# Two-layer hybrid decoder trunk on one core: order of the seven products of the down-projection, place of its residual loads and one operand, and place of the rotary swap

## The chip, the cores and the metric

The kernel runs on one core of a Trainium2 chip, as one launch. The metric is the device time of the whole kernel in microseconds; lower is better. The engines are named PE (TensorE), DVE (VectorE), ACT (ScalarE), POOL (GpSimd) and SP (SyncE); "issue" of a DMA is the instruction on an engine's queue that starts it.

## The reference

A trunk of two layers on 1024 tokens of width 1024, all in float32. Per layer:

```python
proj = x @ w_in                      # u_pool, q, k, v, xc, gate_b, gate_c, gate_logits
q, k = partial_rope(q), partial_rope(k)   # first 16 of the 64 channels of each head
merged = sigmoid gates x (pool mixer, window attention, short conv)
x = layer_norm(ALPHA * x + merged @ w_o)
up = causal_dwconv(x @ w_up);  a, b = split(up)
x = layer_norm(ALPHA * x + (silu(a) * b) @ w_down)     # D_FF = 2816
```

## The kernel before, in words

Every float32 operand is split into a high and a low part (`split`, L87-94: the high part is a cast on ACT, L90; the low part a subtraction on DVE or POOL, L94), and every product is three matmuls (L110, L111, L112). The large matrix products are done in the Winograd form of Strassen's scheme, with seven half-size products in place of eight. Matmuls are 128 x 128 by 128 x 512.

The order of PE and SP is the written one. DVE, ACT and POOL are put in order by a scheduler that weighs priorities; `with self.urgent()` raises the priority of what is issued in it. Buffers come from pools with a fixed count of slots by name (X 14, t 6, s 3, pt 3, q 1, ws 3, w 6): a tile waits until the last reader of its slot is done.

`project` (the in-projection) runs pairs of output blocks, `pair` (L690). Each pair is `begin` (two of its seven products of 12 matmuls) and `rest` (five). In a pair, ACT copies products out of PSUM for the combinations: L724 copies product 1 before product 3 goes on in the same bank, L749 and L753 copy products 3 and 4, L756 product 5. L735 and L738 on POOL make the weight combinations. At the end `then` gets the two finished blocks. For keys and queries `then` is `turn` (L376): it puts `rotate` one tick later and `parts` two ticks later (`later`, ticks counted in pairs, `due` called after `begin`). `rotate` (L336) copies the block on ACT (L340), moves 8 rows four times with DMAs on ACT's queue (L342, L343) and does three operations on DVE (L344 to L346). Pairs of queries hold two such blocks.

`feed_forward` does the up-projection pairs, writes the hidden state to DRAM as the seven left operands of the down-projection (`h_blocks`, POOL and SP queues), then calls `down` (L823). `down` has seven products A11, A12, S2, S1, S3, S4, A22 (`plan`), each of 11 steps `j`, each step of 4 query blocks `q` with 3 matmuls. `operands` loads one step's 256 KB of h_blocks and its weights on SP into staging tiles that go round ws, X, s, makes differences on POOL in S2 (L861 to L863, kept for later products; `t2` is kept for A22) and splits. S1 and S3 use what S2 kept. A22 loads a weight and subtracts it from `t2` on POOL (L871). In the sixth and seventh product odd steps have their low part made on POOL. Steps late in A22 are held and run block by block at the end, so that the first block ends early.

Four banks `bank_a` hold A11 and then S2, S3, A22, four banks `bank_x` A12, S1, S4. After each product `reads` adds its banks into the residual rows `y` (eight tiles of 128 tokens by 1024 in float32, loaded from DRAM, L919, in one go after A11's step 6). Even token tiles are complete after S4, odd ones after A22; `finish` (L932) then calls `norm` (L262: statistics L259 and L267 on DVE, L290 on DVE, L291 on ACT, L292 on POOL or DVE). In layer 0 the normalised tiles are transposed by PE (`to_first`, `to_second`, L298 and following) as operands of the next projection, through the list `pend`; in layer 1 they are stored.

## Time and profile before

| | |
|---|---|
| time, median of 3 runs | 2821.2 us (2819.21 to 2821.59) |
| profiled execution | 2816.18 us, span 2814.4 us |
| granted PE clock, mean | 0.959 |
| busy share PE / DVE / POOL / ACT | 92% / 67% / 52% / 44% |
| DMA | 389.59 MB, mean 138 GB/s |
| first matmuls of the products, layer 0 (A11, A12, S2, S1, S3, S4, A22) | 1145.9, 1191.2, 1221.1, 1260.3, 1290.2, 1320.1, 1350.1 us |
| the same, layer 1 | 2545.1, 2592.1, 2622.0, 2661.1, 2691.1, 2721.0, 2757.8 us |
| first matmul of the second projection; last matmul of all | 1418.7; 2804.7 us |

Times within the trace count from the start of the span. A row of a stretch gives its length, each engine's busy time with the count of its instructions, the clock that the throttle granted to PE (1 is full speed), the mean busy share of the 16 DMA engines and what they moved. A row of waits names the waiting instruction, the one that released it, the sum, the count and the longest.

### The profile page before, as it was taken

What the parts mean: (1) busy time and instruction counts of PE and PEld (TensorE: products, weight loads), DVE (VectorE), ACT (ScalarE), POOL (GpSimd) and SP (SyncE); (2) the same over time, 40 slices, a digit from 0 to 9 for tenths busy, and PEclk for the clock granted to TensorE, in tenths of its full rate; (3) what the DMA queues carried; (4) which work ended last, traced back from release to release, by engine and by line L of the source; (5) the groups of instructions that cost most, each with busy time, mean ns of one, the idle gap of its engine ahead of it and who ended that gap; (6) DMA issues with size and microseconds to landing.
All of it is one profiled execution on the core that took longest, in us unless ns stands there. A gap on an engine that the chain in (4) does not pass through costs nothing.

```text
span 2814.4 us, 31939 instructions
## 1 busy us (share of the span) xinstructions
PE 2596.4 (92%) x11408; PEld 2118.0 (75%) x11408; DVE 1876.6 (67%) x2273; ACT 1228.1 (44%) x2005; POOL 1466.5 (52%) x959
## 2 busy tenths in 40 slices
PE   5989999999899999899689899989988999998996
PEld 4867887787688887678478678877876888876784
DVE  6465556747887877585474755567478887774847
ACT  4434445523544554334344344445235455543333
POOL 3444555666366655171643534666664556641723
PEclk7989999999999999999799999999999999998998
DMA  3433348554133333665223333575632333337552
GB/s 120 136 98 105 120 166 229 164 177 163 57 102 112 113 106 112 239 209 168 98 90 116 103 105 106 206 210 158 205 120 75 99 107 102 113 105 257 198 168 98
DMA packets 162896, 389.59 MB, mean 138 GB/s; under 512 B 17024, under 2 KB 48512, under 8 KB 161712
## 3 DMA queue, kind: packets, MB, share of 16 engines
q1 hardware_dynamic: 136496, 293.02, 32.2%
q0 software_dynamic: 14944, 55.19, 6.8%
q10 hardware_dynamic: 11296, 39.35, 3.7%
q8 instruction: 89, 1.46, 0.2%
q14 instruction: 71, 0.58, 0.1%
HBM read 281.75 MB, written 104.43 MB: 137 GB/s over the span
## 4 chain that ended last, share of the span: by engine, by line
PE 31%; DVE 7%; issue 4%; POOL 4%; ACT 2%; DMA 2%; SPq 0%; ACTq 0%; DVEq 0%; POOLq 0%
PE b L111 10%; PE b L112 10%; PE b L110 10%; DVE w L94 1%; DVE X L94 1%; ACT s L507 1%; DVE ve L275 1%; ACT w L90 0%; POOL ws L735 0%; POOL X L861 0%; POOL w L94 0%; ACT X L90 0%; POOL X L863 0%; DVE st L259 0%; DVE m L498 0%
## 5 line engine op out<-in xcount | busy, mean ns | idle before, releaser
L110 PE MATMUL b<-X,w 128*128 128x512 f32 x2552 | 1016.4, 398 | 56.9 <-ACT s L724 18.5
L112 PE MATMUL b<-X,w 128*128 128x512 f32 x2552 | 1009.6, 396 | 27.6 <-DVE w L94 19.3
L111 PE MATMUL b<-X,w 128*128 128x512 f32 x2552 | 1008.0, 395 | 3.4 <-DVE X L94 3.2
L94 DVE TENSOR_TENSOR w<-ws,w 128x512 fp32r<-128x512 f32 (+1 forms) x449 | 466.8, 1043 | 357.4 <-ACT w L90 342.9
L90 ACT CAST w<-ws 128x512 fp32r<-128x512 f32 (+1 forms) x605 | 409.0, 682 | 484.3 <-PE b L112 161.4
L110 PEld LDWEIGHTS b<-X,w 128*128 128x128 f32 x2552 | 488.8, 192 | 169.3 <-ACT s L724 21.9
L112 PEld LDWEIGHTS b<-X,w 128*128 128x128 f32 x2552 | 487.9, 191 | 135.7 <-DVE w L94 22.5
L111 PEld LDWEIGHTS b<-X,w 128*128 128x128 f32 x2552 | 488.8, 192 | 106.6 <-DVE X L94 5.8
L94 POOL TENSOR_TENSOR w<-ws,w 128x512 fp32r<-128x512 f32 (+1 forms) x156 | 307.4, 1973 | 427.5 <-ACT w L90 425.3
L738 POOL TENSOR_TENSOR ql<-ws 128x512 f32<-128x512 f32 x82 | 125.2, 1527 | 348.9 <-DMA ws<-in_w_in 256.5
L111 PE MATMUL b<-w,w 128*128 128x512 f32 x528 | 215.3, 408 | 37.4 <-DVE w L94 29.6
L110 PE MATMUL b<-w 128*128 128x512 f32 x528 | 212.2, 402 | 28.2 <-ACT w L90 28.2
L112 PE MATMUL b<-w,w 128*128 128x512 f32 x528 | 211.6, 401 | 0.0
L94 DVE TENSOR_TENSOR w<-X,w 128x512 fp32r<-128x512 f32 (+1 forms) x106 | 114.6, 1102 | 84.6 <-ACT w L90 80.6
L111 PEld LDWEIGHTS b<-w,w 128*128 128x128 f32 x528 | 102.9, 195 | 69.0 <-DVE w L94 39.2
L735 POOL TENSOR_TENSOR ws<-ws,ws 128x512 f32<-128x512 f32 x82 | 141.8, 1729 | 5.9
L110 PEld LDWEIGHTS b<-w 128*128 128x128 f32 x528 | 102.8, 195 | 52.4 <-ACT w L90 30.3
L800 DVE SCALAR_TENSOR_TENSOR q<-t,par,q 128x1023 f32<-128x1023 f32 x88 | 126.8, 1441 | 16.2 <-ACT q L797 15.1
L90 ACT CAST w<-X 128x512 fp32r<-128x512 f32 (+1 forms) x110 | 75.5, 704 | 130.3 <-PE b L112 63.9
L735 POOL TENSOR_TENSOR ws<-ql,ws 128x512 f32<-128x512 f32 x82 | 123.5, 1507 | 6.3
L800 DVE SCALAR_TENSOR_TENSOR pt<-t,par,pt 128x1023 f32<-128x1023 f32 x88 | 122.1, 1388 | 0.3
L735 POOL TENSOR_TENSOR ws<-ws 128x512 f32<-128x512 f32 x82 | 118.8, 1449 | 5.2 <-DVE w L94 0.7
(247 smaller groups left out, 3760.3 us busy)
## 6 DMA issues: line engine op xcount, KB each, us to landing
ws<-in_w_up SPq DMA_DIRECT2D x88, 512.0 KB
ws<-in_w_in SPq DMA_DIRECT2D x75, 512.0 KB
gates<-t ACTq DMA_DIRECT2D x48, 512.0 KB
ws<-in_w_o SPq DMA_DIRECT2D x40, 512.0 KB
h_blocks<-t SPq DMA_DIRECT2D x80, 256.0 KB
t<-gates SPq DMA_DIRECT2D x32, 512.0 KB
t<-q_parts POOLq DMA_DIRECT2D x64, 256.0 KB, 4.2
h_blocks<-pt SPq DMA_DIRECT2D x60, 256.0 KB
```

The costliest lines, as they stand in the source:

```text
L90: self.nc.scalar.copy(hi, src)
L94: return eng.tensor_tensor(lo, src, hi.bitcast(F32), op=ALU.subtract)
L110: self.nc.tensor.matmul(out, wh, xh, start=start and i == 0, stop=False, skip_group_check=more)
L111: self.nc.tensor.matmul(out, wh, xl, start=False, stop=False, skip_group_check=more)
L112: self.nc.tensor.matmul(out, wl, xh, start=False, stop=stop and i == n - 1, skip_group_check=more)
L275: nc.vector.scalar_tensor_tensor(ve[:], ve[:], r[:], r[:], op0=ALU.mult, op1=ALU.mult)
L507: nc.scalar.activation(p[:, j, 0:nk], pss[j // 2][:, j % 2], AF.Exp, bias=m[:, j:j + 1], scale=SCALE, accum_out=den[:, j:j + 1])
L735: sub = lambda out, x, y: nc.gpsimd.tensor_tensor(out, x, y, op=ALU.subtract)
L738: nc.gpsimd.tensor_tensor(s1[:], a21, a22, op=ALU.add)
L800: nc.vector.scalar_tensor_tensor(y[:, d:], c[:, :S - d], w(k), y[:, d:], op0=ALU.mult, op1=ALU.add)
```

## The change

Seven edits, all in one diff.

1. The rope tables: the negation goes from DVE to ACT, and the three stores of the table rows from POOL's queue to ACT's.
2. `rotate` is cut in two. `swapped` (the ACT copy and the four DMAs) is issued at the end of `rest`; the DVE part two ticks later and `parts` three ticks later. Ticks are now counted in `due`, which is called after each `begin` and after each `rest`. The other delayed calls keep their places, but for the table spread, which comes half a pair sooner.
3. S3 and S4 change places in `plan`: A11, A12, S2, S1, S4, S3, A22. Even token tiles are complete after the fifth product, and their norm is issued there.
4. A22's right operand is made in S1: `t2` minus the weight on POOL, in place, with the weight's load. A22 then loads only h_blocks. The split of an operand in two halves now goes to POOL too in odd steps of the sixth and seventh product.
5. The residual rows are loaded one after each of A12's first eight steps, and the add of A11's banks into them comes after A12's step 9.
6. The transposes of even tiles are issued at S3's steps 4, 6, 8 and 10 (layer 0), the stores of even tiles at A22's steps 1 to 4 (layer 1).
7. The statistics of an odd tile's second half are taken after S3, and only those of its first half after A22.

The core of the diff:

```diff
-        nc.vector.tensor_scalar(tab[:, 2, :], tab[:, 1, :], -1.0, None, op0=ALU.mult)
+        nc.scalar.mul(tab[:, 2, :], tab[:, 1, :], -1.0)
...
-            nc.gpsimd.dma_start(rows[i].rearrange("f (c j) -> (f c) j", j=64), tab[:, i, :])
+            nc.scalar.dma_start(rows[i].rearrange("f (c j) -> (f c) j", j=64), tab[:, i, :])
...
         def turn(c, put):
-            free = []
-            later(1, lambda: free.append(self.rotate(c, *self.tab)))
-            later(2, lambda: put(*self.parts(free[0], c)))
+            swp = self.swapped(c)
+            self.after(2, lambda: self.rotate(c, swp, *self.tab))
+            self.after(3, lambda: put(*self.parts(swp, c)))
...
-            self.todo.append((1, self.rope_spread))
+            self.after(2, self.rope_spread)
...
             begin()
             self.due()
             rest()
+            self.due()
...
             elif name in ("S1", "S3"):
                 other = kept[j - j % 2][:, j % 2, int(name == "S3"), :]
+                if name == "S1":
+                    t4 = t2[j - j % 4][:, j % 4]
+                    nc.sync.dma_start(st[:, hi], w1[:, lo])
+                    nc.gpsimd.tensor_tensor(t4, t4, st[:, hi], op=ALU.subtract)
...
             else:
-                nc.sync.dma_start(st[:, hi], w1[:, lo])
-                nc.gpsimd.tensor_tensor(st[:, hi], t2[j - j % 4][:, j % 4], st[:, hi], op=ALU.subtract)
+                other = t2[j - j % 4][:, j % 4]
+            e_lo = "gpsimd" if n > 4 and j % 2 else "vector"
             if other is None:
-                self.split(wh, wl, st[:], "scalar", "gpsimd" if n > 4 and j % 2 else "vector")
+                self.split(wh, wl, st[:], "scalar", e_lo)
             else:
-                self.split(wh[:, lo], wl[:, lo], st[:, lo])
-                self.split(wh[:, hi], wl[:, hi], other)
+                self.split(wh[:, lo], wl[:, lo], st[:, lo], "scalar", e_lo)
+                self.split(wh[:, hi], wl[:, hi], other, "scalar", e_lo)
...
-            ("A11", bank_a, True, False, [(0, lo, True, ALU.add)]),
+            ("A11", bank_a, True, False, []),
...
+            ("S4", bank_x, False, True, [(0, hi, False, ALU.add)]),
             ("S3", bank_a, False, True, [(1, hi, False, ALU.add), (1, lo, True, ALU.add)]),
-            ("S4", bank_x, False, True, [(0, hi, False, ALU.add)]),
...
+                if not last and n == 5 and j in (4, 6, 8, 10) or last and n == 6 and j in (1, 2, 3, 4):
+                    self.pending()
...
-                if n == 0 and j == 6:
-                    for t in range(8):
-                        y[t] = self.new([P, D], F32, "pt" if t in (0, 1, 2) else "q" if t == 3 else "t")
-                        nc.sync.dma_start(y[t][:], self.spill1[t])
-                if n == 6 and j == 4:
-                    self.pending()
+                if n == 1 and j < 8:
+                    y[j] = self.new([P, D], F32, "pt" if j in (0, 1, 2) else "q" if j == 3 else "t")
+                    nc.sync.dma_start(y[j][:], self.spill1[j])
+                if n == 1 and j == 9:
+                    for q in range(4):
+                        add(q, 0, lo, bank_a[q][:], True, ALU.add)
...
-                if n >= 5:
-                    self.finish(l, 2 * q + n - 5, y, g, b)
+                if n == 4:
+                    self.finish(l, 2 * q, y, g, b)
+                elif n == 5:
+                    half[q] = self.stats(y[2 * q + 1], (1,))
+                elif n == 6:
+                    self.finish(l, 2 * q + 1, y, g, b, self.stats(y[2 * q + 1], (0,), half[q]))
```

The order of instructions on three engines follows, all from layer 0. First SP before, in A11: the last loads of step 6, the eight row loads (spill), and the first of step 7.

```order
L844 DMA ws_8776<-h_blocks_5256 128x512
L848 DMA ws_8776<-in_w_down 128x512
L919 DMA pt_8795<-spill_67 128x1024
L919 DMA pt_8797<-spill_67 128x1024
L919 DMA pt_8799<-spill_67 128x1024
L919 DMA q_8801<-spill_67 128x1024
L919 DMA t_8803<-spill_67 128x1024
L919 DMA t_8805<-spill_67 128x1024
L919 DMA t_8807<-spill_67 128x1024
L919 DMA t_8809<-spill_67 128x1024
L844 DMA X_8811<-h_blocks_5256 128x512
```

SP now, from A11's step 10 (the first two rows) into A12's first steps:

```order
L852 DMA X_8852<-h_blocks_5256 128x512
L856 DMA X_8852<-in_w_down 128x512
L852 DMA s_8871<-h_blocks_5256 128x512
L858 DMA s_8871<-in_w_down 128x512
L932 DMA pt_8890<-spill_67 128x1024
L852 DMA ws_8892<-h_blocks_5256 128x512
L858 DMA ws_8892<-in_w_down 128x512
L932 DMA pt_8911<-spill_67 128x1024
L852 DMA X_8913<-h_blocks_5256 128x512
L858 DMA X_8913<-in_w_down 128x512
```

All of A11's operand loads now stand ahead of the first row load, and one row load stands between two steps of A12.

POOL before, at the change from S4 to A22: L871 makes A22's operands, L94 the low parts of S4 (w_9994, w_10032) and of A22 (w_10162, w_10202, X_10260), L292 the end of the norm of the four even tiles.

```order
L94 TENSOR_TENSOR w_9994<-X_9992,w_9993 128x1024
L871 TENSOR_TENSOR ws_10220<-X_9219,ws_10220 128x512
L94 TENSOR_TENSOR w_10032<-ws_10030,w_10031 128x1024
L94 TENSOR_TENSOR w_10162<-ws_10160,w_10161 128x1024
L292 TENSOR_TENSOR t_8803<-t_8803,t_9856 128x1024
L292 TENSOR_TENSOR t_8807<-t_8807,t_9856 128x1024
L292 TENSOR_TENSOR pt_8795<-pt_8795,t_9856 128x1024
L292 TENSOR_TENSOR pt_8799<-pt_8799,t_9856 128x1024
L94 TENSOR_TENSOR w_10202<-s_10200,w_10201 128x1024
L871 TENSOR_TENSOR X_10259<-X_9219,X_10259 128x512
L94 TENSOR_TENSOR X_10260<-X_10259,X_10260 128x1024
```

POOL now, from the last of S1's subtractions (L878) to S3: w_9956 and w_9996 are the low parts of S3's steps 1 and 3.

```order
L878 TENSOR_TENSOR X_9326<-X_9326,s_9601 128x512
L878 TENSOR_TENSOR X_9326<-X_9326,ws_9623 128x512
L94 TENSOR_TENSOR w_9956<-X_9954,w_9955 128x512
L94 TENSOR_TENSOR w_9956<-X_9111,w_9955 128x512
L292 TENSOR_TENSOR t_8974<-t_8974,t_9650 128x1024
L292 TENSOR_TENSOR t_9016<-t_9016,t_9650 128x1024
L292 TENSOR_TENSOR pt_8890<-pt_8890,t_9650 128x1024
L292 TENSOR_TENSOR pt_8932<-pt_8932,t_9650 128x1024
L94 TENSOR_TENSOR w_9996<-ws_9994,w_9995 128x512
L94 TENSOR_TENSOR w_9996<-X_9165,w_9995 128x512
```

The four L292 stand in the same place against the next product's step 3, which is S3's now and was A22's; POOL has nothing of S4 any more, and A22's subtractions are behind it.

ACT before, at the first query pair of layer 0, after the two copies L340 (pt_983 and pt_992 are the swapped blocks, s_966 and s_1050 the next pair's copies out of PSUM):

```order
L342 DMA pt_983<-t_844 8x1024
L724 COPY s_966<-b_952 128x512
L343 DMA pt_983<-t_844 8x1024
L342 DMA pt_983<-t_844 8x1024
L343 DMA pt_983<-t_844 8x1024
L342 DMA pt_992<-t_845 8x1024
L753 COPY s_1050<-b_1023 128x512
L343 DMA pt_992<-t_845 8x1024
L342 DMA pt_992<-t_845 8x1024
L343 DMA pt_992<-t_845 8x1024
L90 CAST w_1020<-ws_944 128x512
L749 COPY s_966<-b_952 128x512
```

ACT now at the same place, after the two copies and the four DMAs of the first block (pt_944 and pt_950 are the swapped blocks; L725, L750 and L754 are L724, L749 and L753 of before):

```order
L342 DMA pt_950<-t_851 8x1024
L343 DMA pt_950<-t_851 8x1024
L342 DMA pt_950<-t_851 8x1024
L343 DMA pt_950<-t_851 8x1024
L725 COPY s_978<-b_964 128x512
L90 CAST w_1020<-ws_956 128x512
L90 CAST pt_944<-t_850 128x1024
L90 CAST w_1106<-ws_1104 128x512
L750 COPY s_978<-b_964 128x512
L90 CAST pt_950<-t_851 128x1024
L90 CAST w_1109<-ws_1104 128x512
L754 COPY s_1050<-b_1023 128x512
```

All eight DMA issues now stand ahead of the copy of product 1, the copies of products 3 and 4 stand in the order of the products, and a cast of a rotated block stands ahead of each.

More of the change, by code (lines that the diff above doesn't have):

```diff
@@ L343, in rotate @@
             nc.scalar.dma_start(swp[base + 8:base + 16, :], c[base:base + 8, :])
+        return swp
+    def rotate(self, c, swp, cos, sin):
+        nc = self.nc
         nc.vector.tensor_tensor(c[:], c[:], cos[:], op=ALU.mult)
@@ L346, in rotate @@
         nc.vector.tensor_tensor(c[:], c[:], swp[:], op=ALU.add)
-        return swp
     def parts(self, hi, c):
@@ L403, in keys_first @@
                     self.store(self.vd[:, :, c * HALF:(c + 1) * HALF].rearrange("a p c -> p a c"), t)
-            later(1, keys_first)
             turn(k, put)
+            self.after(2, keys_first)
         def qq(i):
@@ L435, in gate_b @@
                 nc.vector.tensor_tensor(c[i][:], c[i][:], st["y", i][:], op=ALU.mult)
-                later(1, lambda i=i: operand(i, st["y", i], c[i]))
+                self.after(2, lambda i=i: operand(i, st["y", i], c[i]))
         def pooled(*c):
@@ L451, in mapped @@
                     operand(2 + i, self.new([P, S], F32, "pt"), c[i])
-                later(2 + i, mapped)
+                self.after(4 + 2 * i, mapped)
         def gate(n):
@@ L777, in run_pairs @@
             rest()
+            self.due()
         for part in (0, 1):
@@ L782, in run_pairs, with after @@
                 self.due()
+    def after(self, ticks, f):
+        self.todo.append((self.tick + ticks, f))
     def due(self):
-        for n, f in [x for x in self.todo if x[0] <= self.pairs]:
+        self.tick += 1
+        for n, f in [x for x in self.todo if x[0] <= self.tick]:
             f()
-        self.todo = [x for x in self.todo if x[0] > self.pairs]
+        self.todo = [x for x in self.todo if x[0] > self.tick]
     def activated(self, l, f, ca, cb):
@@ L832, in down @@
         kept, t2 = [None] * NJ, [None] * NJ
-        y = [None] * 8
+        y, half = [None] * 8, [None] * 4
         stages = itertools.cycle(("ws", "X", "s"))
@@ L936, in finish @@
             with self.urgent():
-                self.norm(z, g, b, "vector" if t == 7 else "gpsimd")
+                self.norm(z, g, b, "vector" if t == 7 else "gpsimd", st)
             self.pend.append(lambda: self.to_second(y[t - 1], z, t // 2, self.spill[t]) if t % 2
@@ L941, in finish @@
             out = lambda cs: (nc.sync if cs.start else nc.scalar).dma_start(self.out[t, :, cs], z[:, cs])
-            self.norm(z, g, b, "halves", None, out)
+            self.norm(z, g, b, "halves", st, out)
         else:
-            self.norm(z, g, b, "vector")
+            self.norm(z, g, b, "vector", st)
             put = lambda: nc.sync.dma_start(self.out[t], z[:])
```

15 lines of the change are left out of this document (6 added, 9 removed).

## The prediction

> **What bounds the kernel now.** I read the page first, then busy time and granted clock in stretches cut at the seven products of each down-projection and around the two input projections, then what TensorE (PE) waited for in those stretches, and last the timelines of the releasers.
>
> ```profile
> span 2814.4 us, 31939 instructions
> PE 2596.4 (92%) x11408; PEld 2118.0 (75%) x11408; DVE 1876.6 (67%) x2273; ACT 1228.1 (44%) x2005; POOL 1466.5 (52%) x959
> ```
>
> PE is busy for 92% of the span, so only its idle time and its slow clock can be won; the work of the other engines counts only where PE waits for it. The stretches (us, busy of PE, PEld, DVE, ACT, POOL, then clock, DMA share, GB/s) show where that is:
>
> ```profile
> 140.00:250.00 110.00, 94.44 (x370) 75.53 (x369) 70.77 (x63) 41.39 (x65) 51.96 (x35) 0.89 0.37 109
> 250.00:360.00 110.00, 110.00 (x487) 91.10 (x486) 59.98 (x67) 47.63 (x77) 47.88 (x35) 1.00 0.29 98
> 1540.00:1650.00 110.00, 96.44 (x383) 77.35 (x382) 72.52 (x64) 41.77 (x64) 53.56 (x36) 0.91 0.37 110
> 1145.90:1191.20 45.30, 31.98 (x134) 25.73 (x133) 18.16 (x17) 11.41 (x12) 7.79 (x8) 0.85 0.79 289
> 1221.10:1260.30 39.20, 34.51 (x134) 26.34 (x133) 39.06 (x33) 12.66 (x22) 34.90 (x22) 0.91 0.66 231
> 1260.30:1290.20 29.90, 29.90 (x134) 24.76 (x133) 16.82 (x28) 12.57 (x22) 0.00 (x0) 1.00 0.34 103
> 1350.10:1418.70 68.60, 44.43 (x166) 32.08 (x164) 37.68 (x71) 24.42 (x34) 44.12 (x24) 0.78 0.27 92
> 1418.70:1470.00 51.30, 43.09 (x196) 34.92 (x197) 40.77 (x67) 25.20 (x44) 14.37 (x9) 0.87 0.18 69
> 2545.10:2592.10 47.00, 33.38 (x134) 26.69 (x133) 18.14 (x17) 11.88 (x12) 7.78 (x8) 0.82 0.80 290
> 2721.00:2757.80 36.80, 33.26 (x134) 26.15 (x133) 15.17 (x13) 14.35 (x15) 28.72 (x15) 0.91 0.52 173
> 2757.80:2804.70 46.90, 35.18 (x135) 27.50 (x133) 38.42 (x77) 16.25 (x21) 11.77 (x6) 0.85 0.17 68
> ```
>
> From 250 to 360 PE never stops: 110.00 us for 487 matmuls, 0.226 us each. A product of the down-projection has 11 steps of 12 matmuls, 132 in all: 29.8 us, and S1 (1260 to 1290) takes that. Against this measure the stretches lose:
> - projections: 110 - 370 x 0.226 = 26.4 and 110 - 383 x 0.226 = 23.4, **49.8** in both layers;
> - A11: 45.3 - 29.8 = 15.5 and 47.0 - 29.8 = 17.2, **32.7**;
> - S2, layer 0: 39.2 - 29.8 = 9.4, with DVE busy 39.06 of 39.20;
> - the end of layer 0: 68.6 - 29.8 for A22, less 34 short transposes (2 to 8 us, from a quarter of a matmul to a whole one each), about **35**; and 51.3 - 196 x 0.226 = 7.0 at the start of the next projection, or more as far as some of its 196 are short transposes too;
> - the end of layer 1: 7.0 in S4 and 17.1 in A22, **24.1**.
>
> These sum to about 158 us, and are all the change can reach. The waits of PE in the same stretches, in this order (first projection, second, A11 twice, end of layer 0, end of layer 1; total, times, longest):
>
> ```profile
> PE b L110 <- ACT s L724: 8.8, 3, 3.9
> PE b L110 <- ACT s L749: 6.8, 2, 3.5
> ...
> PE b L110 <- ACT s L724: 7.1, 2, 4.4
> PE b L110 <- ACT s L749: 6.5, 2, 3.2
> ...
> PE b L110 <- ACT w L90: 12.9, 1, 12.9
> ...
> PE b L110 <- ACT w L90: 13.2, 1, 13.2
> ...
> PE b L111 <- DVE w L94: 7.2, 1, 7.2
> PE b L110 <- ACT X L90: 6.4, 5, 1.7
> PE b L111 <- POOL w L94: 5.7, 1, 5.7
> PE b L111 <- POOL X L94: 3.4, 3, 1.9
> ...
> PE b L111 <- DVE w L94: 11.7, 3, 9.2
> PE b L111 <- POOL w L94: 2.0, 1, 2.0
> ```
>
> The projections wait 29.2 us in nine stalls and lose 49.8: each us of stall costs 1.7, because the clock stays low behind it (0.89 and 0.91 over the stretch).
>
> **Residual rows (A11 to A12).** SP's own timeline shows why A11 stops:
>
> ```profile
> 1146.11 18.30 SPq L919 DMA_DIRECT2D pt<-spill  x3
> 1164.51 0.40 SPq L919 DMA_DIRECT2D q<-spill  x1
> 1167.49 0.53 SPq L844 DMA_DIRECT2D X<-h_blocks  x1
> ```
>
> The eight row loads sit in SP's queue ahead of A11's step 7; the three into pt stand there from 1146.11 for 18.3 us, one into q and four into t follow, and step 7's operand is issued only at 1167.49. The change puts those four steps ahead of every row load, so the 12.9 and 13.2 us waits lose their cause. What remains of A11 is its hidden states: the last ones are written by GpSimd (POOL) while A11 runs, and step 10 needs them some 27 us after the product starts; I leave nothing for that. The eight loads (0.52 MB each) now go between the steps of A12, each of which loads 0.52 MB itself: 1.05 MB in 2.7 us is 386 GB/s. The DMA engines have shown that once:
>
> ```profile
> 1170.00:1180.00 10.00, 1.66 (x3) 1.06 (x4) 1.91 (x2) 2.23 (x3) 0.00 (x0) 0.50 1.03 393
> ```
>
> So A12 runs at the limit for eight steps with the lead that SP has, and the last three repay it. I take 1.3 us a layer for it, bounds 0 and 5. The four adds into the rows move from A12's start to its step 9; they are the same adds, and S2 needs their banks only after. Term: -32.7 + 2.6 = **-30** (-36 to -20).
>
> **The rotary part (projections).** ACT at the first query pair:
>
> ```profile
> 143.72 1.99 ACT L340 COPY pt<-t 128x1024 f32<-128x1024 f32 x2 [2.14 <-DVE t L760]
> 144.79 0.65 ACTq L342 DMA_DIRECT2D pt<-t  x1
> 145.62 0.58 ACT L724 COPY s<-b 128x512 f32<-128x512 f32 x1
> 153.67 0.59 ACT L753 COPY s<-b 128x512 f32<-128x512 f32 x1 [7.47 <-PE b L112]
> 156.21 0.58 ACT L749 COPY s<-b 128x512 f32<-128x512 f32 x1
> ```
>
> Before, one of the eight issues stood ahead of the copy L724, three stood behind L753, and L753 stood ahead of L749, which PE needs first. Now all eight stand ahead of the copy (L725), and the two late copies are in PE's order. So the first stall grows: seven more issues of 0.65 are 4.6 us, from 2 up to 6.6, or about 4 where the swap copies start sooner, as their vector add no longer queues behind the splits. At the second query pair the copy had slack, and I take 2.5 there. In return the stalls on L749 (3.5 at the longest) go, but for a cast of the rotated tile ahead of each copy (0.5 to 1 each), and so does most of the third stall (3.9), which came from the rotation ending late on DVE. Per query pair 4.5 to 8.6 us, taken 5, against 29.2 / 4 = 7.3: 4 x 2.3 x 1.7 = 16, and 2 for the keys: **-18** (-35 to +10: at 2 a pair 4 x 5.3 x 1.7 = 36 less, at 8.6 a pair 4 x 1.3 x 1.7 = 9 more).
>
> **S1, S3 and A22's operand.** S1 gets a subtraction on POOL per step and its 256 KB load. A step has 2.7 us, and S1's DMA runs at 103 GB/s; 0.26 MB per 2.7 us adds 97. The subtraction itself, and the price of POOL and DVE working together (S2's splits, then S1's):
>
> ```profile
> L871 POOL TENSOR_TENSOR X<-X,X x6: 1271/1770/2287, 1333.2 to 2760.2; 128x512 f32<-128x512 f32 x6
> L94 DVE TENSOR_TENSOR w<-X,w 128x512 fp32r<-128x512 f32 x14 | 22.2, 1616 | 0.1
> L94 DVE TENSOR_TENSOR w<-X,w 128x512 fp32r<-128x512 f32 x15 | 9.9, 686 | 4.3 <-ACT w L90 4.3
> ```
>
> DVE's split takes 1616 ns beside a POOL that never rests (S2) and 686 alone (S1). Per step of the new S1 POOL is busy for 1.8; DVE does 0.42 of its speed in that time, 0.75 of its 1.37 us of work, and the other 0.62 alone: 2.4 of 2.7. So S1 stays at 29.8 by a narrow margin, bounds 0 and 9.4 a layer (S2's loss). By the Trainium skill (GPSIMD Engine Reference, 1. Specifications) the two engines share their SBUF interfaces, with contention where a vector instruction has two SBUF inputs; the subtraction would then never be free beside these splits. The trace agrees (1616 against 686), and by that rule S1 goes to S2's 39.2, which is the bound just named.
>
> **Even tiles one product sooner.** The norm of the even tiles moves from A22's head to S3's, and takes its stalls along: in DVE's and POOL's order S3's steps 2 and 3 stand behind it as A22's did.
>
> ```profile
> 1358.50 6.73 POOL L292 TENSOR_TENSOR t<-t,t 128x1024 f32<-128x1024 f32 x2 [7.42 <-ACT t L291]
> 1365.19 4.68 POOL L292 TENSOR_TENSOR pt<-pt,t 128x1024 f32<-128x1024 f32 x2
> 1369.83 3.32 POOL L94 TENSOR_TENSOR w<-s,w 128x1024 fp32r<-128x1024 f32 x1
> ```
>
> The 7.2 and 5.7 stay, with the slow clock about 18 of A22's 35. What goes is the rest, 17: POOL's subtractions and splits after it (6.4 and 3.4). Against it, A22 now takes the banks that S3 has just filled: eight adds, two a bank, where PE needs a bank each 0.7 us; I take 3. The odd tiles' last norm is as long as before, less four half statistics: 2 at the next projection. Layer 0: -17 + 3 - 2 = **-16** (-30 to -3). Layer 1: of 24.1 the 9.2 stall (13 with its clock) moves to S3, the 7.0 in S4 goes (its odd steps were POOL's, and S4 is now all on DVE), 4 more go in A22, and the bank wait comes: -7 - 4 + 4 = **-7** (-14 to +2).
>
> **At nothing:** the table rows on ACT's queue (three issues of 0.65, long before the tables are read), the spread of the tables ahead of a weight load on SP, gains loaded one product sooner: 0, bounds -2 and +2.
>
> **Sum:** -30 - 18 - 16 - 7 = -71. The profiled run took 2816.2 (span 2814.4, and 1.8 around it), so 2745; it lies 5 under the median of 2821.2, so **2750**. What a measurement of this kernel can tell from no change is 0.2%, 5.6 us.
>
> **Rivals.**
> - *ACT's eight issues eat the projection's gain* (0.18). For: the order puts them ahead of a copy that PE already waited for, and a stall of 6.6 us keeps the clock low. Against: two other stalls per pair lose their cause. Then +9 in place of -18: 2750 + 27 = **2777**.
> - *S2 takes back what A11 gains* (0.08). For: 386 GB/s beside a limit of 393; DVE is full for all of S2, so an operand that comes late is never made up. Then the first S2 loads come no sooner than today and S1 starts when it did: 2750 + 30 = **2780**.
> - *The stalls at S3's head dissolve* (0.12). For: S3 has lighter POOL steps than A22 had, so its operands may be made ahead of the norm. Then the 18 and the 13 go as well: 2750 - 31 = **2719**, and lower still where the projections reach their bound.
> - *Slower: two engines on one memory path set the pace from S1 to A22* (0.04). POOL now works in S1, S3 and A22, three products a layer, 66 steps. At S2's pace (39.2 / 11 = 3.56 us a step) they cost 9.4 each, 56 in all: 2806, still faster. It turns slower where a step takes more than 2.7 + 77 / 66 = 3.9 us, since 77 is the gain plus the 5.6; at 4.0 the time is 2750 + 66 x 1.3 = **2836**. Against: S2 has three subtractions a step on POOL, these products one or two. The rule of the Trainium skill cited above (GPSIMD Engine Reference, 1. Specifications) points this way and gives no price.
> - *The change does less than it says* (0.02): all stalls only change product, 2816 to 2826.
>
> My forecast has 0.56. Its own range is 2725 to 2775; with the first three rivals 2705 to 2795. Faster: 0.56 + 0.18 + 0.08 + 0.12 = 0.94; same 0.02; slower 0.04.
>
> **What would show it.** Right: A11 near 30 us in both layers, no wait for L90 there; A12 30 to 31; S2 still about 39; S1 at 30 with DVE's splits near 1.2 us; a stall of 7 to 10 us at S3's steps 2 and 3 in both layers; A22 near 33; L725 as the projections' main wait, 2.5 to 4 us each. Wrong: A12 or S2 longer by what A11 lost, S1 at 39, L725 stalls over 6 us with the projections still losing 25 a layer, or S3 without its stall.

## The result and the profile after

| | before | after |
|---|---|---|
| median | 2821.39 us (4 runs, 2819.21 to 2824.63) | 2790.53 us (4 runs, 2787.64 to 2791.05) |
| profiled execution | 2816.18, span 2814.4 | 2791.05, span 2789.3 |

The ratio after / before is 0.9888 (95% interval 0.987 to 0.9905): the kernel is faster by 31 us, 1.1%. The forecast was 2750, a gain of 71 us. The sign is right, and the gain is less than half of what the sum said. The time lies outside the forecast's own range (2725 to 2775) and inside the wider one with the rivals (2705 to 2795), near its upper end; that it does so is luck, since none of these rivals came about: several terms missed at once. One execution of swap_half, of 5183.27 us, is left out of the numbers below.

The page of the changed kernel begins:

```profile
span 2789.3 us, 31987 instructions
PE 2586.3 (93%) x11408; PEld 2110.6 (76%) x11408; DVE 1912.6 (69%) x2274; ACT 1230.9 (44%) x2028; POOL 1482.7 (53%) x976
```

The stretches, cut where the products of the changed kernel begin: the two projections, then layer 0 from A11 to A22 in the new order and the start of the next projection, then A11, S2, S1, S3 and A22 of layer 1.

```profile
140.00:250.00 110.00, 94.53 (x401) 75.79 (x400) 71.38 (x68) 44.01 (x69) 56.48 (x37) 0.97 0.37 110
1520.00:1630.00 110.00, 97.14 (x407) 78.19 (x406) 69.58 (x65) 43.12 (x67) 57.98 (x40) 0.95 0.37 110
1144.70:1174.60 29.90, 29.90 (x134) 24.75 (x133) 18.60 (x17) 11.42 (x12) 7.78 (x8) 1.00 0.98 357
1174.60:1204.50 29.90, 29.90 (x134) 24.75 (x133) 19.41 (x15) 11.78 (x13) 17.02 (x10) 1.00 0.72 263
1204.50:1246.80 42.30, 35.45 (x134) 26.32 (x132) 38.49 (x30) 12.82 (x23) 41.31 (x27) 0.92 0.78 266
1246.80:1280.90 34.10, 31.08 (x132) 24.46 (x133) 25.76 (x29) 12.02 (x20) 14.48 (x9) 1.00 0.74 241
1280.90:1310.90 30.00, 30.00 (x134) 24.69 (x133) 15.85 (x18) 11.77 (x13) 1.89 (x2) 1.00 0.19 53
1310.90:1372.00 61.10, 43.12 (x166) 33.84 (x165) 34.66 (x62) 30.07 (x53) 35.95 (x21) 0.79 0.37 119
1372.00:1405.80 33.80, 32.55 (x133) 26.24 (x133) 23.92 (x37) 6.39 (x12) 16.06 (x10) 0.92 0.15 50
1405.80:1457.00 51.20, 42.52 (x204) 33.43 (x203) 40.86 (x66) 26.80 (x45) 16.02 (x10) 0.93 0.20 69
2529.80:2559.70 29.90, 29.90 (x134) 24.75 (x133) 18.60 (x17) 11.43 (x12) 7.79 (x8) 1.00 0.97 350
2589.60:2632.60 43.00, 34.34 (x134) 23.95 (x132) 35.52 (x30) 12.99 (x23) 42.37 (x28) 1.00 0.77 268
2632.60:2666.70 34.10, 31.15 (x132) 24.48 (x133) 25.71 (x29) 11.93 (x20) 14.41 (x9) 1.00 0.68 232
2696.70:2747.30 50.60, 34.91 (x134) 27.41 (x133) 44.85 (x62) 28.53 (x49) 31.36 (x19) 0.85 0.30 99
2747.30:2779.30 32.00, 32.00 (x131) 26.15 (x131) 19.33 (x41) 3.19 (x5) 0.00 (x0) 0.92 0.08 33
```

A11 takes 29.9 in both layers (it took 45.3 and 47.0), and A22 is short. But S2, S1 and S3 are longer than before: 42.3, 34.1 and 61.1 in layer 0, where they took 39.2, 29.9 and 29.9. S3 is now the longest product of the kernel, at a granted clock of 0.79.

In the projections 401 and 407 matmuls run in the stretches that held 370 and 383. By the measure of the prediction (0.226 us each) they lose 19.4 and 18.0 where they lost 26.4 and 23.4. The waits of PE in the changed kernel, in the first projection, the second, S3 of layer 0 and the end of layer 1 (total, times, longest):

```profile
PE b L110 <- ACT s L725: 11.2, 4, 5.9
PE b L110 <- ACT s L754: 4.3, 2, 3.0
...
PE b L110 <- ACT s L725: 10.3, 4, 5.3
PE b L110 <- ACT s L754: 2.6, 2, 1.9
...
PE b L111 <- POOL w L94: 6.7, 1, 6.7
PE b L111 <- DVE w L94: 5.5, 2, 5.1
PE b L110 <- ACT w L90: 4.6, 2, 3.4
...
PE b L111 <- DVE w L94: 8.0, 1, 8.0
PE b L110 <- DVE pt L895: 4.0, 1, 4.0
PE b L111 <- POOL w L94: 3.7, 2, 2.7
```

The copy behind the eight DMA issues (L725) is the projections' main wait. In sum PE waits no less there than before: 28.4 us in twelve stalls (15.5 and 12.9), where it was 29.2 in nine; what is higher is the granted clock, 0.97 and 0.95 where it was 0.89 and 0.91. S3 has three waits where the forecast had two. With the n-th matmul of one trace set against the n-th of the other (both have 11408), the 25 us of the profiled runs (2814.4 - 2789.3) are made up so:

| where | forecast | measured |
|---|---|---|
| A11, both layers | -32.7 | -32.5 |
| A12 and S2 (row loads) | +2.6 | +7.0, all in S2 |
| S1, both layers | 0 | +8.4 |
| layer 0, S3 + S4 + A22 | -14 | -3.6 |
| start of the second projection (its first 51 us) | -2 | -1.8 |
| layer 1, S3 + S4 + A22 | -7 | -0.5 |
| both projections | -18 | -12 |
| the rest, nearly all between the projections and A11 | 0 | +10 |

The medians are 31 us apart and these two executions 25; the execution of the kernel before lies 5 us under its median.

### The profile page after: what moved, and what is told of

Same layout as the page of the kernel before. It is cut to its first block, busy times and chain, and to the rows that moved or that the text cites. A ratio compares the mean times of both kernels' runs of the same rounds, so it can differ in the third digit from the quotient of the medians.

```text
span 2789.3 us, 31987 instructions
## 1 busy us (share of the span) xinstructions
PE 2586.3 (93%) x11408; PEld 2110.6 (76%) x11408; DVE 1912.6 (69%) x2274; ACT 1230.9 (44%) x2028; POOL 1482.7 (53%) x976
## 5 line engine op out<-in xcount | busy, mean ns | idle before, releaser
L94 DVE TENSOR_TENSOR w<-ws,w 128x512 fp32r<-128x512 f32 (+1 forms) x449 | 456.0, 1019 | 347.3 <-ACT w L90 335.2
L90 ACT CAST w<-ws 128x512 fp32r<-128x512 f32 (+1 forms) x605 | 407.0, 678 | 481.8 <-PE b L112 156.6
L94 POOL TENSOR_TENSOR w<-ws,w 128x512 fp32r<-128x512 f32 (+1 forms) x156 | 300.4, 1928 | 417.3 <-ACT w L90 417.0
L94 DVE TENSOR_TENSOR w<-X,w 128x512 fp32r<-128x512 f32 (+1 forms) x101 | 125.7, 1263 | 43.9 <-ACT w L90 43.4
L736 POOL TENSOR_TENSOR ws<-ws,ws 128x512 f32<-128x512 f32 x82 | 145.5, 1775 | 5.9
L90 ACT CAST w<-X 128x512 fp32r<-128x512 f32 (+1 forms) x118 | 79.4, 691 | 112.6 <-PE b L112 66.9
L736 POOL TENSOR_TENSOR ws<-ql,ws 128x512 f32<-128x512 f32 x82 | 124.9, 1523 | 6.3
```

Source lines behind the costliest of these rows:

```text
L90: self.nc.scalar.copy(hi, src)
L94: return eng.tensor_tensor(lo, src, hi.bitcast(F32), op=ALU.subtract)
L736: sub = lambda out, x, y: nc.gpsimd.tensor_tensor(out, x, y, op=ALU.subtract)
```

## The experiments

The runs shared three medians of the kernel before: 2820.56 (sub_s4, late_tr, swap_later, odd_rows_s1), 2821.55 (three, three_spread, swap_half, rot_old) and 2819.66 (rows_only, order_old, spread_calm, all_five). Except where it is said otherwise an edit is made to the changed kernel, and "after" is its 2790.53.

The theory: the gain is A11's alone; S1 pays for eleven GpSimd subtractions that come at once, S2 for row loads that come too early, and S3 for transposes that came along with the early norm. The rivals: these losses are of one cause (the memory path, or the DMA limit), or are only late effects of a stall in front.

**sub_s4: A22's operand made in S4, not in S1.** The subtraction and its load move from a product in which DVE splits POOL's results to one that had little work, with a staging tile of their own.

```diff
-                if name == "S1":
-                    t4 = t2[j - j % 4][:, j % 4]
-                    nc.sync.dma_start(st[:, hi], w1[:, lo])
-                    nc.gpsimd.tensor_tensor(t4, t4, st[:, hi], op=ALU.subtract)
...
+                t4 = t2[j - j % 4][:, j % 4]
+                b1 = self.new([P, 1024], F32, next(stages))
+                nc.sync.dma_start(b1[:, lo], w1[:, lo])
+                nc.gpsimd.tensor_tensor(t4, t4, b1[:, lo], op=ALU.subtract)
```

> The changed kernel with the subtraction of A22's last operand, and its load, moved from S1 to S4 (a staging tile of its own there). In the changed kernel S1 takes 34.0 and 34.1 us in place of 29.9. Theory (VectorE's splits are slowed by the eleven GpSimd subtractions that run back to back at S1's head): S1 returns to 30 in both layers, S4, where VectorE has 1.2 us of work in a step of 2.7, stays at 30 to 31, and the time is 2790 - 8 = 2782. Rival (S1 starts slowly because S2's differences and bank adds end late, whatever GpSimd does then): S1 stays at 33 to 34, time 2790.

Measured: 2769.93 (2766.82 to 2774.53), ratio 0.9823 (0.9806 to 0.984), 20.6 less than after. First what S1 of the changed kernel shows. POOL's groups around its start, in 1240 to 1262 us (busy, mean ns, idle before), and DVE's in 1250 to 1262:

```profile
L878 POOL TENSOR_TENSOR X<-X,s 128x512 f32<-128x512 f32 x4 | 7.0, 1740 | 0.0
L878 POOL TENSOR_TENSOR X<-X,ws 128x512 f32<-128x512 f32 x4 | 6.5, 1622 | 0.0
L878 POOL TENSOR_TENSOR X<-X,X 128x512 f32<-128x512 f32 x3 | 5.3, 1756 | 0.0
...
L94 DVE TENSOR_TENSOR w<-X,w 128x512 fp32r<-128x512 f32 x6 | 8.2, 1410 | 0.0
L94 DVE TENSOR_TENSOR w<-ws,w 128x512 fp32r<-128x512 f32 x1 | 1.8, 1775 | 0.0
L94 DVE TENSOR_TENSOR w<-s,w 128x512 fp32r<-128x512 f32 x1 | 1.8, 1772 | 0.0
```

The eleven subtractions (4 + 4 + 3) run back to back, 18.8 us with no idle time, and DVE's splits beside them take 1410 to 1775 ns with none of its own. Then S1 and S4 of layer 0 and S1 of layer 1 with the work moved:

```profile
1245.70:1275.60 29.90, 29.90 (x134) 24.76 (x133) 19.19 (x26) 12.37 (x21) 9.46 (x7) 1.00 0.73 234
1275.60:1305.60 30.00, 30.00 (x133) 24.66 (x132) 17.15 (x18) 11.73 (x14) 8.95 (x7) 1.00 0.45 146
...
2617.80:2647.70 29.90, 29.90 (x134) 24.75 (x133) 18.91 (x26) 12.36 (x21) 9.34 (x7) 1.00 0.75 241
```

S1 is back at 29.9 in both layers and S4 pays nothing. That is 8.4 us, the 8 of the theory; the other 12 were not expected. S4, S3 and A22 of layer 0 take 7.2 less together, nearly all of it in S3 (54.6 in place of 61.1). There DVE makes one more step's splits (w<-ws, w<-X) before that of the transposed tile (X<-b), and stands idle for 8.0 and 7.7 us in place of the 18.2 that the next run is about:

```profile
1324.31 1.69 DVE L94 TENSOR_TENSOR w<-ws,w 128x512 fp32r<-128x512 f32 x1 [8.03 <-issue]
...
1335.42 1.29 DVE L94 TENSOR_TENSOR X<-b,X 128x512 fp32r<-128x512 f32 x2 [7.74 <-ACT X L90]
```

Why the scheduler chose this order is not shown. Of what is left, 2 us lie in the same three products of layer 1, and 3 between layer 1's projection and its A11, where the two kernels have the same instructions in the same order; more of that below.

**late_tr: the even tiles' transposes of layer 0 in A22 (steps 1 to 4), not in S3.**

```diff
-                if not last and n == 5 and j in (4, 6, 8, 10) or last and n == 6 and j in (1, 2, 3, 4):
+                if n == 6 and j in (1, 2, 3, 4):
```

> The changed kernel with the transposes of the even tiles in layer 0 issued at A22's steps 1 to 4 in place of S3's steps 4, 6, 8, 10. In the changed kernel S3 of layer 0 takes 61.1 us, and VectorE stands idle for 18.2 us in it, waiting for a cast of a transposed tile. Theory (the transposed tiles' splits stand ahead of S3's operands on ACT and VectorE, and wait for the norm): S3 of layer 0 falls to 46 to 50 us, A22 gives 2 to 5 of it back, time 2778 to 2782. Rival (the norm's last step on GpSimd is what S3 waits for, and the transposes only fill the same hole): S3 loses less than 4 us and A22 takes as much, time 2790.

Measured: 2782.19 (2779.47 to 2783.75), ratio 0.9865 (0.985 to 0.9881), 8.3 less. What S3 of the changed kernel does at its head, by the timelines of DVE, ACT and POOL (start, length, engine, line, and in brackets the idle time before it and its releaser):

```profile
1321.05 0.69 DVE L94 TENSOR_TENSOR w<-X,w 128x512 fp32r<-128x512 f32 x1
1339.96 1.39 DVE L94 TENSOR_TENSOR X<-b,X 128x512 fp32r<-128x512 f32 x2 [18.22 <-ACT X L90]
1341.27 2.36 DVE L94 TENSOR_TENSOR w<-X,w 128x512 fp32r<-128x512 f32 x2
...
1339.34 1.22 ACT L90 CAST X<-b 128x512 fp32r<-128x512 f32 x2 [9.73 <-PE b L298]
...
1319.33 6.96 POOL L292 TENSOR_TENSOR t<-t,t 128x1024 f32<-128x1024 f32 x2 [7.77 <-ACT t L291]
1326.25 4.64 POOL L292 TENSOR_TENSOR pt<-pt,t 128x1024 f32<-128x1024 f32 x2
```

DVE stands idle for 18.2 us, though S3's later operands are its to make. In its order the split of the transposed tile (X<-b) stands ahead of them; that split waits for ACT's cast, the cast for PE's transposes (L298), and these for step 4, whose way goes through steps 2 and 3 and POOL's norm. With the transposes one product later S3 and A22 are:

```profile
1307.70:1355.50 47.80, 35.30 (x134) 28.11 (x133) 23.56 (x49) 18.74 (x32) 24.95 (x15) 0.82 0.30 99
1355.50:1395.50 40.00, 36.20 (x166) 28.90 (x165) 36.23 (x44) 17.53 (x33) 25.81 (x16) 0.96 0.17 58
```

S3 loses 13.3 of its length and A22, with 32 more instructions on PE, gets 6.2 back. The net of 7.1 is about what the other order on DVE gave in sub_s4 (7.2), with the transposes still in S3. The 47.8 that is left is 17.9 above a product without a stall (29.9), the 18 that the forecast put there for the norm itself.

**swap_later: the swap, the rotation and the parts one tick later each.**

```diff
-            swp = self.swapped(c)
-            self.after(2, lambda: self.rotate(c, swp, *self.tab))
-            self.after(3, lambda: put(*self.parts(swp, c)))
+            swp = []
+            self.after(2, lambda: swp.append(self.swapped(c)))
+            self.after(3, lambda: self.rotate(c, swp[0], *self.tab))
+            self.after(4, lambda: put(*self.parts(swp[0], c)))
```

> The changed kernel with the swap of each key and query block (copy and four DMAs on ACT's queue), its rotation and its parts one tick later each: the swap stands behind the next pair's first copy, L725. In the changed kernel PE waits 6.0, 2.9, 5.4 and 2.6 us at L725 behind query pairs. Theory (the eight DMA issues ahead of that copy are what it waits for): these four stalls go, no other copy of the pair is late, 17 us of stalls with some clock, time 2768 to 2775. Rival (the later rotation makes the later copies, or the gates' activations, late, as in the kernel before): stalls of 3 to 4 us come at two other places of each query pair, time 2785 to 2795.

Measured: 2793.63 (2786.73 to 2795.64), ratio 0.99 (0.9883 to 0.9917): no gain on after, as the rival had it. The first projection's waits are now a copy of product 1 (L726, 7.2 us in two) and of product 3 (L751, 6.4 in two, the longest 3.2): the stalls behind the eight issues are exchanged for the kind that the kernel before had.

**odd_rows_s1: the rows of odd tiles loaded in S1, those of even tiles at A12's even steps.**

```diff
-                if n == 1 and j < 8:
-                    y[j] = self.new([P, D], F32, "pt" if j in (0, 1, 2) else "q" if j == 3 else "t")
-                    nc.sync.dma_start(y[j][:], self.spill1[j])
+                if n in (1, 3) and j in (0, 2, 4, 6):
+                    i = j + n // 2
+                    y[i] = self.new([P, D], F32, "pt" if i in (0, 1, 2) else "q" if i == 3 else "t")
+                    nc.sync.dma_start(y[i][:], self.spill1[i])
```

> The changed kernel with the residual rows of the odd tiles loaded in S1 (steps 0, 2, 4, 6), where they are first needed, and only those of the even tiles in A12. In the changed kernel S2 takes 42.3 and 42.9 us, 39.2 and 39.1 before, and GpSimd's chain of differences starts 12.5 us after A12's first matmul, 9.0 before. Theory (the row loads delay S2's first loads, and the chain of 56 us passes that on): the chain starts 9 to 10 us after A12, S2 takes 39 to 40, time 2784. Rival (S2 is set by VectorE and GpSimd sharing a path, and the loads do not matter): S2 stays at 42, time 2790.

Measured: 2780.96 (2778.46 to 2782.45), ratio 0.9861 (0.9846 to 0.9876), 9.6 less. POOL's first subtraction for S2 in layer 0 and SP's issue of the load that it waits for, in the kernel before (the subtraction alone), in the changed kernel, and with fewer rows in A12:

```profile
1200.16 1.29 POOL L861 TENSOR_TENSOR X<-s 128x512 f32<-128x512 f32 x1 [37.27 <-DMA s<-in_w_down]
```

```profile
1181.14 0.33 SPq L862 DMA_DIRECT2D s<-in_w_down  x1
...
1187.25 1.83 POOL L869 TENSOR_TENSOR X<-s 128x512 f32<-128x512 f32 x1 [25.57 <-DMA s<-in_w_down]
```

```profile
1178.10 0.33 SPq L862 DMA_DIRECT2D s<-in_w_down  x1
...
1181.84 1.28 POOL L869 TENSOR_TENSOR X<-s 128x512 f32<-128x512 f32 x1 [21.86 <-DMA s<-in_w_down]
...
1202.80:1242.50 39.70, 34.30 (x134) 25.32 (x132) 39.56 (x30) 13.09 (x23) 38.95 (x25) 0.96 0.81 295
2582.00:2621.50 39.50, 33.52 (x134) 23.89 (x132) 37.53 (x30) 13.01 (x23) 38.95 (x25) 1.00 0.85 292
```

POOL waits for the weights of S2, which stand in SP's queue behind the rows. It starts 12.7 us after A12 began (1174.6) in the changed kernel and 8.9 after it (A12 from 1172.9) here; before, it was 9.0. The load is issued 6.5 us after A12 began in place of 5.2, and takes 6.1 us from its issue to POOL's start in place of 3.7, so that more of the delay lies in the transfers under way than in the order of issue; S2 goes from 42.3 and 43.0 to 39.7 and 39.5, its length before the change (39.2 in layer 0).

**three: sub_s4, late_tr and odd_rows_s1 in one kernel**, with the three diffs above.

> The changed kernel with the three edits of before together: the subtraction in S4, layer 0's transposes of even tiles in A22, the odd tiles' rows loaded in S1. Theory (the three losses lie in S1, in S3 and in S2, and have nothing to do with each other): the gains add, 20.6 + 8.3 + 9.6 = 38 by the medians, time 2752, with S1 at 30, S2 at 39.7, S3 of layer 0 at 47. Rival (they overlap, since each only moves work to a hole that another one fills, S4's GpSimd against S3's head): less than 25 of it, time 2765 or more.

Measured: 2763.6 (2760.23 to 2766.52), ratio 0.9797 (0.9781 to 0.9813), 27 less than after, where the three alone took off 20.6, 8.3 and 9.6, 38.5 together. They overlap, by more than the theory and less than the rival had it. In layer 0, S4, S3 and A22 together give 7.2 in sub_s4, 7.1 in late_tr and 11.2 here: S3 is 47.8, as with the transposes moved alone, so sub_s4's gain there is part of the same loss. The greater part of the overlap lies between layer 1's projection and its A11: against the kernel before, that stretch is 3.8 us longer in the changed kernel, 1.0, 1.4 and 0.4 in the three alone, and 4.0 here. All five have the same instructions there in the same order, so this part of the three gains, 8.6 us in sum, comes of no instruction that the edits touch.

**three_spread: as three, and the even tiles' norms at S3's steps 1, 3, 5 and 7, not all at its head.**

```diff
+                if n == 5 and j in (1, 3, 5, 7):
+                    self.finish(l, j - 1, y, g, b)
...
-                if n == 4:
-                    self.finish(l, 2 * q, y, g, b)
-                elif n == 5:
+                if n == 5:
```

> The kernel with the three edits, and the norms of the four even tiles not issued in one block after S4 but one at a time after S3's steps 1, 3, 5 and 7, in both layers. Theory (what is left of S3's loss, 18 us in layer 0 and 20 in layer 1, is the block of four norms ahead of S3's operands of steps 2 and 3 on VectorE, ACT and GpSimd): S3 falls to 31 to 36 in both layers, A22 stays within 3 us, time 2752 - 28 = 2724. Rival (the work of the norms is the loss, not its block: each norm stalls one step by 3 to 4 us): S3 at 42 or more, time 2740 to 2750.

Measured: 2757.48 (2753.38 to 2758.87), ratio 0.9773 (0.9758 to 0.9788), 6 less than three. Half of the theory held: S3 of layer 1 fell from 49.1 to 39.4, but in layer 0 it stayed at 48.4. There `finish` raises the priority of the norm, and the scheduler put the four together again: POOL's four L292 stand between 1308.7 and 1324.2 us with one split among them.

**spread_calm: as three_spread, without the raised priority for even tiles.**

```diff
-            with self.urgent():
-                self.norm(z, g, b, "vector" if t == 7 else "gpsimd", st)
+            if t % 2:
+                with self.urgent():
+                    self.norm(z, g, b, "vector" if t == 7 else "gpsimd", st)
+            else:
+                self.norm(z, g, b, "gpsimd", st)
```

> The kernel with the three edits and the spread norms, and the raised priority taken from the even tiles' norms in layer 0. With it, S3 stayed at 48.4 us in layer 0 (47.8 without the spread), while in layer 1, which has no raised priority there, it fell from 49.1 to 39.4. Theory (the raised priority puts the norms back in one block ahead of S3's operands): S3 of layer 0 falls to 38 to 41, time 2748. Rival (in layer 0 it is the norm's last step on GpSimd, 2.4 to 3.5 us a tile, that S3's odd steps wait for): S3 stays at 45 or more, time 2755.

Measured: 2742.63 (2740.14 to 2745.21), ratio 0.9728 (0.9715 to 0.9741), 14.9 less than three_spread. S3 of layer 0 and of layer 1:

```profile
1300.70:1339.80 39.10, 32.25 (x134) 25.57 (x133) 33.44 (x50) 18.67 (x31) 25.52 (x15) 0.96 0.40 128
...
2662.80:2702.20 39.40, 31.32 (x134) 24.74 (x133) 37.89 (x57) 27.87 (x49) 26.00 (x17) 0.96 0.42 134
```

The same norms cost 9 us in S3 in place of 18 in layer 0 and 19 in layer 1. In layer 1 the spacing did it alone (three_spread); in layer 0 it took the spacing and the normal priority together, and the normal priority without the spacing was not run.

**rot_old: the rotary part as before** (swap and rotation in one piece two ticks after the block, the parts four).

```diff
-            swp = self.swapped(c)
-            self.after(2, lambda: self.rotate(c, swp, *self.tab))
-            self.after(3, lambda: put(*self.parts(swp, c)))
+            swp = []
+
+            def whole():
+                swp.append(self.swapped(c))
+                self.rotate(c, swp[0], *self.tab)
+
+            self.after(2, whole)
+            self.after(4, lambda: put(*self.parts(swp[0], c)))
...
-            turn(k, put)
...
+            turn(k, put)
```

> The changed kernel with the swap and rotation of keys and queries as they were before (in one piece, one half-pair later, the parts one half-pair later); the table stores and the down-projection as changed. Theory (the rotary part gains 6.8 and 5.3 us in the two projections, and nothing of it is lost elsewhere): time 2790 + 12 = 2802. Rival (it is given back in the stretches after the projections, where the changed kernel takes 5 us a layer more than before): 2790 to 2794.

Measured: 2791.7 (2789.37 to 2798.3), ratio 0.9899 (0.9882 to 0.9917): within 1.2 us of after. Yet its projections lose what they lost before the change (372 and 385 matmuls in the 110 us stretches, 25.9 and 23.0 us lost). So the new form does save 12 us there, and in the whole kernel they do not show; where they are missing is taken up at the end.

**swap_half: only the second query block's swap, rotation and parts one tick later**; the first block and the keys as in the changed kernel.

```diff
-        def turn(c, put):
-            swp = self.swapped(c)
-            self.after(2, lambda: self.rotate(c, swp, *self.tab))
-            self.after(3, lambda: put(*self.parts(swp, c)))
+        def turn(c, put, k=0):
+            if k:
+                swp = []
+                self.after(2, lambda: swp.append(self.swapped(c)))
+            else:
+                swp = [self.swapped(c)]
+            self.after(2 + k, lambda: self.rotate(c, swp[0], *self.tab))
+            self.after(3 + k, lambda: put(*self.parts(swp[0], c)))
...
-                    turn(c[j], put)
+                    turn(c[j], put, j)
```

> The changed kernel with only the second query block of each pair treated one tick later (copy, four DMAs, rotation, parts), so that one copy and four DMA issues stand ahead of L725 in place of two and eight. Theory (the wait at L725 is the time of what stands ahead of it on ACT): the waits of 6.0 and 5.4 us fall by 3 to 3.6, those of 2.9 and 2.6 go, and no other stall comes, time 2778. Rival (a later second block makes the third stall of the pair come back, as when both were later): time 2787 to 2793.

Measured: 2781.15 (2770.47 to 2783.25), ratio 0.985 (0.983 to 0.987), about 9 less than after. The first projection's waits for the copies are 9.1 us in three, the longest 3.9, against 15.5 in six; 428 matmuls run in its 110 us. The stall behind the first copy falls as expected, from 5.9 to 2.6: four issues ahead of a copy are a shorter stall than eight. That no other would be left was not so (2.5 and 3.9).

**rows_only: the kernel before, with edit 5 alone.**

```diff
-            ("A11", bank_a, True, False, [(0, lo, True, ALU.add)]),
+            ("A11", bank_a, True, False, []),
...
-                if n == 0 and j == 6:
-                    for t in range(8):
-                        y[t] = self.new([P, D], F32, "pt" if t in (0, 1, 2) else "q" if t == 3 else "t")
-                        nc.sync.dma_start(y[t][:], self.spill1[t])
+                if n == 1 and j < 8:
+                    y[j] = self.new([P, D], F32, "pt" if j in (0, 1, 2) else "q" if j == 3 else "t")
+                    nc.sync.dma_start(y[j][:], self.spill1[j])
+                if n == 1 and j == 9:
+                    for q in range(4):
+                        add(q, 0, lo, bank_a[q][:], True, ALU.add)
```

> The kernel before with one part of the change alone: the residual rows loaded one by one in A12, the add of A11's banks after A12's step 9. Theory (this part removes the two stops of 13 us in A11 with their clock, 32.5 us, and costs S2 3 us a layer; all other parts of the change together come to about nothing): 2821 - 26 = 2795, A11 29.9 in both layers, S2 42. Rival (the other parts carry a third or more of the 31 us, this one less, as S2 or the ends of the layers take it back): 2802 or more.

Measured: 2794.12 (2786.99 to 2796.6), ratio 0.9907 (0.9891 to 0.9922), 25.5 less than before. Its A11 and S2 of layer 0:

```profile
1150.90:1180.80 29.90, 29.90 (x134) 24.76 (x133) 18.62 (x17) 11.41 (x12) 7.79 (x8) 1.00 0.96 344
1210.70:1253.30 42.60, 34.62 (x134) 25.49 (x133) 35.13 (x32) 12.65 (x22) 37.66 (x25) 0.96 0.68 231
```

One of the seven edits gives 25.5 of the 30.9 us of the whole change, with the gain in A11 and the loss in S2 that the whole change has. The other six together bring 4 to 5.

This kernel has the instructions of the kernel before, in the same order on every engine, up to A11. Even so its A11 begins at 1150.9 in the execution shown, and at 1145.9 in that of the kernel before. Its first projection:

```profile
140.00:250.00 110.00, 92.38 (x372) 74.10 (x372) 69.67 (x63) 41.76 (x64) 52.16 (x36) 0.92 0.36 110
```

PE waits 17.7 us there where it waited 15.6, its clock is 0.92 and not 0.89, and 372 matmuls run in place of 370. So two executions of the same instructions can differ by 5 us before A11, and a difference of that size at one place of two traces shows nothing.

**order_old: S3 before S4 again** (edits 3, 6 and 7 undone, the others kept).

```diff
-            ("S4", bank_x, False, True, [(0, hi, False, ALU.add)]),
             ("S3", bank_a, False, True, [(1, hi, False, ALU.add), (1, lo, True, ALU.add)]),
+            ("S4", bank_x, False, True, [(0, hi, False, ALU.add)]),
...
-                if n == 4:
+                if n == 5:
                     self.finish(l, 2 * q, y, g, b)
-                elif n == 5:
-                    half[q] = self.stats(y[2 * q + 1], (1,))
```

> The changed kernel with S3 ahead of S4 again: even tiles complete after the sixth product, their transposes and stores are issued where they were before, and an odd tile's statistics are taken at once after A22. The subtraction stays in S1, the rows in A12. Theory (completing the even tiles one product sooner only moves the stalls of their norm from A22 to S3): S3, S4 and A22 of layer 0 sum to 121 to 129 us (125 in the changed kernel), time 2786 to 2796. Rival (the earlier norm is worth what it was forecast to be, 15 us in layer 0 and 7 in layer 1): time 2805 or more.

Measured: 2783.6 (2779.79 to 2786.67), ratio 0.9873 (0.9859 to 0.9886). This is 6.9 us faster than the whole change by the medians, and 5.2 with each set against the kernel before as it was timed with it. Its last product of layer 0, which has the norms and the transposes at its head again:

```profile
1337.10:1397.50 60.40, 41.71 (x166) 31.59 (x164) 47.93 (x78) 24.94 (x44) 38.97 (x22) 0.83 0.22 79
```

The row takes in the first matmul of the next projection and the wait of 1.7 behind it; up to that matmul A22 takes 58.5. With S3 and S4 at 29.9 each the three make 118.3, where the changed kernel's three make 30.0 + 61.1 + 33.8 = 124.9; in layer 1 they make 108.9 and 113.6. In the changed kernel the even tiles come a product sooner and the end comes later.

**all_five: spread_calm and swap_half in one kernel.**

> The kernel of spread_calm with the second query block of each pair treated one tick later, as in swap_half. Theory (the projections' 9.4 us have nothing to do with the down-projections): 9 us under spread_calm. Rival (they overlap as the rotary part's gain did, by waits that come back later): less than 4 us under spread_calm.

Measured: 2735.99 (2733.27 to 2737.88), ratio 0.9704 (0.9691 to 0.9718), the fastest of all: 6.6 less than spread_calm, between the two expectations. Its profiled execution has a span of 2733.3 us.

## Why the prediction was right in its sign and wrong in its size

- **Residual rows: right.** A11 gave 32.5 of a forecast 32.7, and the waits of 12.9 and 13.2 are gone. A12 lost nothing, though the row loads stand in it.
- **What the rows cost: mis-sized, and in another product.** The 2.6 laid on A12 was 7.0 in S2. The argument counted the bytes of A12's own steps; S2's first weights stand in the same queue behind the rows, and POOL's chain of subtractions, busy for 41.3 of S2's 42.3 us, began 3.7 us later against A12's start (12.7 against 9.0 before). The rival "S2 takes back what A11 gains" named the place, with 30 us as the price; it took under a quarter of that. odd_rows_s1 shows the cause: with half the rows in A12 the chain and S2 are back where they were.
- **S1: the step failed.** "Per step of the new S1 POOL is busy for 1.8" spread the subtractions over the product. Nothing holds POOL to PE's steps: the operands' loads were there, and all eleven ran at once, against DVE's first splits. S1 lost 4.2 us in each layer, of a bound of 9.4 a layer. The rule of the Trainium skill (GPSIMD Engine Reference, 1. Specifications: vector instructions with two SBUF inputs contend with GpSimd) pointed the right way, and this trace agrees: 1410 to 1775 ns beside POOL, against 686 alone. It held for the 19 us in which both were at work, not for the whole product.
- **The ends: the step that failed most.** "What goes is the rest, 17" for layer 0: it did not go. The norm's 18 was right (17.9 in late_tr), but the term has no price for the transposes, which edit 6 takes into S3 with the norm. Their splits, ahead of the product's own operands in DVE's order, added 13.3 there, 7.1 of it net; sub_s4 had the same 7 with the transposes left in S3 and another order on DVE, which points at the order and not at the work. A22 became short as forecast (33.8 for "near 33"). In layer 1 S3 lost 20.7 where the forecast moved 13 there; spreading the norms took 9.7 of it away. Together the ends gave 4.1 where 21 had been forecast, and order_old shows that the order of before, with the other edits, is 5 to 7 us better.
- **The rotary part: mis-sized, and its price per stall is not a constant.** L725's stalls were 5.9 and 5.3 at the longest, within the 4 to 6.6 that the eight issues bound, and the projections gained 12 for a forecast of 18 or a rival's loss of 9. The forecast took 2.3 us of waiting off a query pair, at 1.7 for each. The two executions compared do not show that: the waits are 28.4 us for 29.2, and the gain came with the clock. Over more traces the waits of the first projection do fall, to 11.6 to 15.5 us in eight kernels with the new rotary part from 15.6 to 18.5 in three with the old one (before, rows_only, rot_old). The price was 1.7 in the kernel before, but 17.7 us of waits cost 25.9 in rows_only, 1.5 each, and 15.5 cost 19.4 in the changed kernel, 1.3 each.
- **Whether the rotary part is worth something over the whole kernel stays open.** rot_old says 1 us. Between the projections and A11 the changed kernel lost 5.4 us in layer 0 and 3.8 in layer 1 against the kernel before, among them a wait of 4.0 us at 1835 to 1839 us for a cast of an attention tile on ACT (L90). These losses are no effect of the new form that the runs show. rows_only, with the instructions of the kernel before, lost 5.9 in the same part of layer 0, and seven kernels with the instructions of the changed one lost 1.8 to 5.4. In layer 1 they lost 0.2 to 4.5, and waited 0.8 to 4.0 for that cast. So executions of the same instructions differ by as much, and the one of the kernel before was a fast one. In rot_old's trace 4.5 us come from S4, S3 and A22 of layer 0 (120.4 in place of 124.9), for which no cause is shown.

The forecast's sum took every term at its own place. Three of the four things moved (rows, subtraction, norms) cost more where they landed than the sum had set: the first two were priced at or near zero there, the third as in its old place and without the transposes that came along.

## What to carry to other kernels

A block of work that is moved one product earlier brings all that hangs on it, and lands in front of something on each in-order engine; look up in the order what stands behind it there (here splits of transposes ahead of the next operands, 18 us of idle DVE), and spread it over the steps that have room before moving it. An engine that is ahead of its readers doesn't spread its work: price it at the moment its inputs arrive, all at once. Compare two traces place by place, and where the instructions are the same, hold the difference against a second execution before you give it a cause. And try the parts of a change alone: here one edit gave 25 of 31 us, and the others together, made gentler and with the row loads spread over two products, another 58 (2794.1 to 2736.0).

## What the runs showed of the hardware

The DMA engines held what the prediction feared for. In A12's first 12.4 us PE never stopped while rows and operands came at 395 GB/s:

```profile
1174.60:1187.00 12.40, 12.40 (x56) 10.26 (x55) 6.91 (x8) 5.28 (x5) 0.00 (x0) 1.00 1.05 395
```

The cost of this burst fell on what came after it: the first weights of S2 were issued 1.3 us later and took 2.4 us longer, and S2 lost 3.1 and 3.9 us. The other surprise is how far the price of the same work depends on its spacing: four norms at the head of S3 cost 18 us with a clock of 0.82, and spread over seven steps, without the raised priority in layer 0, 9 us with a clock of 0.96.
